# One forget gate, one conditioning step and one buffer: three re-orderings in a two-layer decoder trunk

## The chip, the cores and the metric

The kernel runs on one core of a Trainium2 chip. The metric is the device time of one execution in microseconds (us). The kernel before takes 3213.15 us, the median of three runs from 3211.61 to 3214.26. Engines are named as the profile names them: PE is TensorE (PEld its weight loads), DVE is VectorE, ACT is ScalarE, POOL is GpSimd, SP is SyncE, which issues most transfers ("SPq" is its queue).

## The reference

Two residual layers over a sequence of 512 tokens of width 1024, conditioned on a vector c. All data are fp32.

```
for layer in range(2):
    mod = silu(c) @ ada_w[layer] + ada_b[layer]        # 1024 x 6144
    sh1, sc1, g1, sh2, sc2, g2 = split(mod, 6)
    h = rmsnorm(x, norm_mix[layer]) * (1 + sc1) + sh1
    y = even_mixer(h) if layer == 0 else odd_mixer(h)
    x = x + g1 * y
    h = rmsnorm(x, norm_ffn[layer]) * (1 + sc2) + sh2
    x = x + g2 * peer_ffn(h)                           # 8 heads, 128 x 128 experts, top 16
out = rmsnorm(x, norm_final)

def odd_mixer(h):                                      # forgetting attention, 16 heads of 64
    q, k, v, f = split_cols(h @ w_in, (1024, 1024, 1024, 16))
    F = cumsum(log_sigmoid(f + b_forget))              # along the tokens
    s[t, u] = q[t] . k[u] / 8 + F[t] - F[u]            # causal
    return softmax(s) @ v @ w_out
```

The even mixer (sparse attention beside differential attention) and the expert stage are computed as well; of the expert stage only the first step, the normed and modulated input h, is touched by the change.

## The kernel before, in words

The 512 tokens are four blocks of 128 (NTB). A matmul of fp32 data is made as three products of fp32r pieces: `mm3` (L147 to L149) multiplies hi by hi, lo by hi and hi by lo. A tile is split into its pieces by `split_to`: ACT writes hi (L161, L164 with a scale) and DVE writes lo (L162, L165). In the profile wh and wl are the pieces of a weight chunk, kh, kl, qh, ql those of keys and queries, pth and ptl those of the transposed softmax.

**The ring.** The pool "stream" has three slots of 128x1024 under one tag, raw. Weight chunks (512 KB, L169, named raw), the slices of ada_w (256 KB, L237, named araw), the transposed forget logits fT, the triangle tri and a few others all take the next slot of this ring, so a load on SP's queue waits until an earlier user has let a slot go.

**The order of the work.** The program is written as generators. A list scheduler then sets the order on each engine, by its own estimates of when an instruction can start; the order in the code is where it starts from, not what it ends with.

**The odd mixer** (function `odd`) does this, in turn: the first half of v (1600 to 1644 us of the span); the forget logits (`proj_s` with chunk W[24], to 1650 us); the forget gate's chain: fT out of PSUM (L1002), four transposes (L1005), z = f + b (L1009), u = |z| (L1012), Exp (L1013), Ln (L1014), z again (L1015), the cumulative sum as four matmuls with a triangle of -1 (L1020), its split cum (L1022, L1023); then the second half of v with the chunks W[20] to W[23] (`proj_m`, 96 matmuls of 128x512, to 1682 us); then the attention, 1682 to 1898 us; then `mixer_out`, the output projection and the first steps of the expert stage.

**The attention** has 64 units, one for each of 16 heads and 4 token blocks, written out in four steps (`head_unit`): the scores (names sc), the causal mask (L1056, on DVE), the maximum mx (L474, DVE) and the exponential e (L477, ACT); the division (rc on DVE at L482, e at L808 on ACT); the transposes (tr, L495, PE) with pth (L497, ACT) and ptl (L500, DVE); and after the fourth block the product with v (pp) and oT (L818, ACT). Between the units `run_units` draws steps of two fillers: the projection of the q and k of the next pairs of heads, two 512 KB chunks for each group of eight units, and the list `bg`, from which it draws OB steps for each unit. In the odd mixer bg holds 64 steps of `ada` (L223 to L247): four of the six 1024-wide parts of mod, each as two halves of eight slices of ada_w. A step loads a slice (L237) and adds it, weighted, to adacc on DVE (L239 for a first slice, L241 for the others); after eight steps four matmuls (L245) sum adacc over the partitions and DVE writes mod (L247). With OB = 2 the steps are drawn in the first 32 of the 64 units.

**The expert stage's input.** For each token block `norm_block` writes xn (L299, with rstd from L288 to L290), and `h_steps` (L322) makes the modulated input: per half of the width four PE transposes (L330) of xn into PSUM, four scalings into hfull (L335 on ACT for b = 0 and 2, L337 on DVE for b = 1 and 3), and the split of hfull into h2h and h2l. hfull has one buffer, so a block waits for the split of the one before it. This happens at the end of mixer_out in both layers, ahead of the expert stage's first matmuls (named ups).

Of the kernel before, what the change touches and what calls it, by code (L numbers as in the profile page):

```python
# [7 lines left out]
F32 = mybir.dt.float32  # L8
# [9 lines left out]
P = 128  # L18
D = 1024
T = 512  # L20
# [41 lines left out]
OP = 1.8  # L62
OB = 2
OPP = 3
# [45 lines left out]
class Trunk:  # L110
    def __init__(self, tc, ctx, I, out):
        self.tc, self.nc, self.ctx, self.I, self.out = tc, tc.nc, ctx, I, out
        self.n = 0
        self.done = set()
        self.bg = []
        self.uw = []
        self.pin = False
        self.own = {}
        self.pending = {}
        self.banks = {"pp": 4, "sc": 2, "tr": 2, "s": 2, "u": 2, "g": 2, "q": 2, "ada": 1}  # L120
# [200 lines left out]
    def h_steps(self, tb, xn, cols, hT, pool, psum, tag):  # L321

        nc = self.nc
        a, sh = cols
        full = pool.tile([P, KT, P], F32, tag="hfull", name=self.nm("hfull"), bufs=1)
        for half in range(2):
            ps = self.bank(psum, tag)
            for b in range(4):
                kt = half * 4 + b
                nc.tensor.transpose(ps[:, b * P:(b + 1) * P], xn[:, kt * P:(kt + 1) * P], self.ident)  # L330
            for b in range(4):
                kt = half * 4 + b
                s = slice(b * P, (b + 1) * P)
                if b % 2 == 0:
                    nc.scalar.activation(full[:, kt], ps[:, s], AF.Identity, bias=sh[:, kt:kt + 1], scale=a[:, kt:kt + 1])  # L335
                else:
                    nc.vector.tensor_scalar(full[:, kt], ps[:, s], a[:, kt:kt + 1], sh[:, kt:kt + 1],  # L337
                                            op0=ALU.mult, op1=ALU.add)
            yield
            k = slice(half * 4, half * 4 + 4)  # L340
            t = slice(tb * P, (tb + 1) * P)
            self.split_to(hT[0][:, k, t], hT[1][:, k, t], full[:, k])
            yield
        return full
# [616 lines left out]
    def odd(self, layer):  # L961
        nc, I = self.nc, self.I
        W = I["odd_w"]
        with ExitStack() as s2:
# [28 lines left out]
            ep = s2.enter_context(self.pool("ep"))  # L993
            self.e_bufs = OEB
            with self.pool("fp") as fp:
                ps = self.bank(psum, "pp")
# [7 lines left out]
                for tb in range(NTB):  # L1004
                    nc.tensor.transpose(pf[:, tb * 16:(tb + 1) * 16], fT[:, tb * P:(tb + 1) * P], self.ident[:16, :16])  # L1005
                bf = fp.tile([P, 16], F32, name="bf")
                nc.scalar.dma_start(bf, I["odd_b_forget"].to_broadcast([P, 16]))
# [7 lines left out]
                nc.vector.scalar_tensor_tensor(z, z, 0.0, u, op0=ALU.min, op1=ALU.subtract)  # L1015
                tri = self.stream.tile([P, D], F32, tag="raw", name=self.nm("tri"))
                nc.sync.dma_start(tri[:, :T], I["ntri"])
                ps = self.bank(psum, "tr")
# [7 lines left out]
            def proj_qk(i):  # L1026
# [9 lines left out]
                for j in range(2):  # L1036
# [3 lines left out]

            self.proj_m([W[20 + c] for c in range(4)], hT, psum,
                        lambda tb, ps: self.split_to(vs[1][0][:, tb], vs[1][1][:, tb], ps))
            sq.close()
# [173 lines left out]
    def peer_enter(self, layer):  # L1217
# [9 lines left out]
        self.cols = self.mod_cols(layer, 1, self.hp)  # L1227
        self.xn = {}
        self.ssx = self.hp.tile([P, NTB, 2], F32, name=self.nm("ssx"))
        self.pad(self.hp, 96)  # L1230
# [15 lines left out]
    def peer(self, layer, last):  # L1246
# [7 lines left out]
        with ExitStack() as s1:  # L1254
            psum = s1.enter_context(self.pool("rps", bufs=2, space=PSUM))
            gls[0] = self.u_block(layer, 0)
            w = self.load_split(I["peer_wq"][layer, 0])
            self.peer_h(NDT, psum, "g")
            self.sn.close()
            for n in range(1, FIRST):  # L1260
# [315 lines left out]
```

## Time and profile before

| what | value |
|---|---|
| median of three runs | 3213.15 us (3211.61 to 3214.26) |
| profiled execution | 3209.09 us, its span 3206.9 us |
| mean granted TensorE clock | 0.988 |
| busy share of the span | PE 97%, DVE 80%, ACT 43%, POOL 22% |
| forget gate's chain | 1650 to 1660 us |
| attention of the odd mixer | 1682.3 to 1898.2 us |
| even mixer_out, end with h | to 375 us |
| odd mixer_out, end with h | to 1949 us |

The times of the trace are counted from the first instruction. A busy share is that of instructions in work on an engine. The granted clock is 1.00 at 2.4 GHz and 0.50 at 1.2 GHz, and a stretch between these values holds both. A row with "[idle before <-X]" names what the engine waited for.

### The profile page before, as it was taken

Reading aid. Unit: us, or ns where it says so; the run is one execution under the profiler, and the core shown is the slowest. Engines: PE = TensorE matmul, PEld = TensorE weight load, DVE = VectorE, ACT = ScalarE, POOL = GpSimd, SP = SyncE. Lnnn points to the kernel's source line nnn. Section 1 sums busy time; section 2 is a strip of 40 time slices with the busy share of each in tenths; the row PEclk is TensorE's granted clock in tenths of the full one; section 3 lists DMA queues with packets and bytes.
Section 4 is the critical chain, followed back from the end, with each engine's and each line's share of the span. In section 5 each row is a group of like instructions: output and inputs, shape, how many; then the busy total and the mean of one; then the engine's idle time right before and its main releaser. Section 6 shows DMA issues by size and latency. Waiting matters only on the chain.

```text
span 3206.9 us, 45322 instructions
## 1 busy us (share of the span) xinstructions
PE 3106.1 (97%) x16416; PEld 2689.4 (84%) x16416; DVE 2576.4 (80%) x5096; ACT 1367.1 (43%) x2276; POOL 705.8 (22%) x564
## 2 busy tenths in 40 slices
PE   8999899999999999999989999999999999999998
PEld 4766788998899999987867778899989999899877
DVE  6987799997687778788758767999867877778787
ACT  5567423553333333333445663255533333333333
POOL 0000000002344444434210000000024444444331
PEclk9999999999999999999999999999999999999999
DMA  7415523658799999999724422255688999999895
GB/s 242 132 60 178 173 86 107 228 224 289 269 334 322 319 336 333 317 329 320 238 101 159 138 86 79 92 178 224 214 289 296 332 327 324 322 320 319 311 324 196
DMA packets 304193, 758.92 MB, mean 237 GB/s; under 512 B 24456, under 2 KB 125376, under 8 KB 297824
## 3 DMA queue, kind: packets, MB, share of 16 engines
q1 hardware_dynamic: 225248, 480.04, 43.5%
q0 software_dynamic: 74240, 268.54, 23.2%
q10 hardware_dynamic: 4480, 7.44, 0.7%
q8 instruction: 129, 2.11, 0.3%
q14 instruction: 96, 0.79, 0.1%
HBM read 698.96 MB, written 56.64 MB: 236 GB/s over the span
## 4 chain that ended last, share of the span: by engine, by line
PE 67%; DVE 14%; DMA 13%; issue 3%; ACT 2%; POOL 0%; SPq 0%; DVEq 0%; ACTq 0%; POOLq 0%
PE ups L149 9%; PE ups L147 9%; PE ups L148 9%; PE y L148 8%; PE y L149 8%; PE y L147 8%; DMA gv<-in_peer_v_dram,eidx 5%; PE pp L147 3%; PE pp L149 3%; PE pp L148 3%; DMA araw<-in_ada_w_dram 2%; DVE wl L162 2%; DMA raw<-in_peer_v_dram 2%; PE gps L1210 1%; DMA gu<-in_peer_u_dram,eidx 1%
## 5 line engine op out<-in xcount | busy, mean ns | idle before, releaser
L161 ACT ACTIVATE wh<-raw 128x1024 fp32r<-128x1024 f32 x598 | 631.7, 1056 | 1007.8 <-PE ups L148 449.0
L162 DVE TENSOR_TENSOR wl<-raw,wh 128x1024 fp32r<-128x1024 f32 x598 | 729.5, 1220 | 140.0 <-ACT wh L161 139.0
L149 PE MATMUL ups<-h2h,wl 128*128 128x384 f32 x2048 | 693.7, 339 | 4.3 <-DVE wl L162 4.3
L147 PE MATMUL ups<-h2h,wh 128*128 128x384 f32 x2048 | 694.5, 339 | 3.1 <-ACT gl L1087 2.4
L148 PE MATMUL ups<-h2l,wh 128*128 128x384 f32 x2048 | 690.8, 337 | 0.0
L1447 POOL DMA_INDIRECT gu<-in_peer_u_dram,eidx x256 | 288.5, 1127 | 1637.6 <-DVE eidx L1306 1181.0
L147 PE MATMUL y<-wh,weh 128*128 128x512 f32 x1536 | 601.0, 391 | 11.3 <-ACT weh L161 9.4
L148 PE MATMUL y<-wl,weh 128*128 128x512 f32 x1536 | 603.7, 393 | 5.8 <-DVE wl L162 5.7
L149 PE MATMUL y<-wh,wel 128*128 128x512 f32 x1536 | 602.4, 392 | 0.0
L1447 POOL DMA_INDIRECT gv<-in_peer_v_dram,eidx x256 | 392.3, 1532 | 533.5 <-DVE gu L1454 333.5
L1462 DVE SCALAR_TENSOR_TENSOR acc<-gv,act,acc 128x1024 f32<-128x1024 f32 x256 | 328.2, 1282 | 165.7 <-DMA gv<-in_peer_v_dram,eidx 165.2
L147 PEld LDWEIGHTS ups<-h2h,wh 128*128 128x128 f32 x2048 | 386.6, 189 | 11.0 <-ACT gl L1087 3.0
L149 PEld LDWEIGHTS ups<-h2h,wl 128*128 128x128 f32 x2048 | 386.1, 189 | 7.5 <-DVE wl L162 7.5
L148 PEld LDWEIGHTS ups<-h2l,wh 128*128 128x128 f32 x2048 | 386.8, 189 | 6.5
L147 PEld LDWEIGHTS y<-wh,weh 128*128 128x128 f32 x1536 | 289.4, 188 | 71.1 <-ACT weh L161 10.7
L1454 DVE SCALAR_TENSOR_TENSOR gu<-gu,htm 128x1024 f32<-128x1024 f32 x256 | 312.1, 1220 | 45.2 <-DMA gu<-in_peer_u_dram,eidx 44.6
L148 PEld LDWEIGHTS y<-wl,weh 128*128 128x128 f32 x1536 | 289.2, 188 | 69.0 <-DVE wl L162 11.3
L161 ACT ACTIVATE weh<-wf 128x384 fp32r<-128x384 f32 x256 | 133.7, 524 | 497.9 <-PE y L148 356.9
L149 PEld LDWEIGHTS y<-wh,wel 128*128 128x128 f32 x1536 | 289.2, 188 | 61.2 <-DVE wel L162 1.3
L162 DVE TENSOR_TENSOR wel<-wf,weh 128x384 fp32r<-128x384 f32 x256 | 141.5, 553 | 82.0 <-ACT weh L161 81.7
L1341 DVE TENSOR_TENSOR wf<-gl,gt 128x384 f32<-128x384 f32 x256 | 140.2, 552 | 10.2 <-DMA gt<-gates 9.6
L1213 ACT ACTIVATE gst<-gps 128x512 f32<-128x512 f32 x192 | 104.1, 596 | 40.2 <-PE gps L1211 31.2
(411 smaller groups left out, 4272.0 us busy)
## 6 DMA issues: line engine op xcount, KB each, us to landing
raw<-in_peer_uT_dram SPq DMA_DIRECT2D x256, 512.0 KB
raw<-in_peer_v_dram SPq DMA_DIRECT2D x256, 512.0 KB
araw<-in_ada_w_dram SPq DMA_DIRECT2D x192, 256.0 KB
gates<-gst SPq DMA_DIRECT2D x48, 1024.0 KB
gt<-gates SPq DMA_DIRECT2D x32, 1536.0 KB
raw<-in_peer_wq_dram SPq DMA_DIRECT2D x32, 512.0 KB
raw<-in_odd_w_dram SPq DMA_DIRECT2D x25, 512.0 KB
raw<-in_even_w_dram SPq DMA_DIRECT2D x23, 512.0 KB
```

The source lines that it names most:

```text
L147: mm(out, a[0], b[0], start=start, stop=False)
L148: mm(out, a[0], b[1], start=False, stop=False)
L149: mm(out, a[1], b[0], start=False, stop=stop)
L161: self.lact = nc.scalar.activation(hi, src, AF.Copy)
L162: self.last = nc.vector.tensor_tensor(lo, src, hi.bitcast(F32), op=ALU.subtract)
L1210: nc.tensor.matmul(ps[:, z], oh[:, t, 1], og[:, t, 0], start=True, stop=False)
L1213: nc.scalar.activation(st[:, :, lt:lt + 4], ps.rearrange("p t i -> p i t"), AF.Copy, scale=1.0 / GSC)
L1341: nc.vector.tensor_tensor(wf.rearrange("p (c t) -> p c t", t=CT), gls[i].rearrange("p (c t) -> p c t", t=CT), self.gt[:, :, i % IG], op=AL ...
L1447: nc.gpsimd.indirect_dma_start(out=r, out_offset=None, in_=table, in_offset=bass.IndirectOffsetOnAxis(ap=eidx[:, k:k + 1], axis=0))
L1454: nc.vector.scalar_tensor_tensor(r, r, 1.0, htm, op0=ALU.mult, op1=ALU.mult, accum_out=act[:, k:k + 1])
L1462: nc.vector.scalar_tensor_tensor(acc, r, act[:, j:j + 1], acc, op0=ALU.mult, op1=ALU.add)
```

## The change

First, `proj_m` of the second half of v becomes a generator, `more`; the code draws VFILL = 14 of its steps between the gate's last z and the triangle matmuls, and the rest behind them. The load of the triangle is issued ahead of the gate's chain. A step of this generator holds three matmuls, one mm3. Second, OB is 1, so the 64 conditioning steps are drawn one a unit in all 64 units of the odd attention. Third, hfull has two buffers while the expert stage's input is made, in both layers, and under the same condition the scaling with b = 1 goes to ACT as well: three of four on ACT, one on DVE.

```diff
-OB = 2
+OB = 1
+VFILL = 14
...
+        self.hf_bufs = 1
...
-        full = pool.tile([P, KT, P], F32, tag="hfull", name=self.nm("hfull"), bufs=1)
+        full = pool.tile([P, KT, P], F32, tag="hfull", name=self.nm("hfull"), bufs=self.hf_bufs)
...
-                if b % 2 == 0:
+                if b % 2 == 0 or b < self.hf_bufs:
                     nc.scalar.activation(full[:, kt], ps[:, s], AF.Identity, bias=sh[:, kt:kt + 1], scale=a[:, kt:kt + 1])
                 else:
                     nc.vector.tensor_scalar(full[:, kt], ps[:, s], a[:, kt:kt + 1], sh[:, kt:kt + 1],
...
+            more = self.proj_m_steps([W[20 + c] for c in range(4)], hT, psum,
+                                     lambda tb, ps: self.split_to(vs[1][0][:, tb], vs[1][1][:, tb], ps))
             with self.pool("fp") as fp:
...
+                tri = self.stream.tile([P, D], F32, tag="raw", name=self.nm("tri"))
+                nc.sync.dma_start(tri[:, :T], I["ntri"])
                 bf = fp.tile([P, 16], F32, name="bf")
...
                 nc.vector.scalar_tensor_tensor(z, z, 0.0, u, op0=ALU.min, op1=ALU.subtract)
-                tri = self.stream.tile([P, D], F32, tag="raw", name=self.nm("tri"))
-                nc.sync.dma_start(tri[:, :T], I["ntri"])
+                for _ in range(VFILL):
+                    next(more)
                 ps = self.bank(psum, "tr")
...
-            self.proj_m([W[20 + c] for c in range(4)], hT, psum,
-                        lambda tb, ps: self.split_to(vs[1][0][:, tb], vs[1][1][:, tb], ps))
+            for _ in more:
+                pass
...
         self.xn = {}
+        self.hf_bufs = 2
...
             self.peer_h(NDT, psum, "g")
+            self.hf_bufs = 1
             self.sn.close()
```

Two lines more in the helpers and up to seven in `odd` shift the line numbers: L149 of before is L151, L161 is L163, L241 is L243, L1020 is L1027 and L1056 is L1063 in the changed kernel.

On PE, at the forget gate, before: the transposes of the logits, the four triangle matmuls (16x512 to 16x128), and then the first of the second half of v (wh_15673 is the piece of W[20]).

```order
L1005 MATMUL tr_15642<-ident,fT_15640 128x16 x4
L1020 MATMUL tr_15658<-tri_15656,z 16x512
L1020 MATMUL tr_15658<-tri_15656,z 16x384
L1020 MATMUL tr_15658<-tri_15656,z 16x256
L1020 MATMUL tr_15658<-tri_15656,z 16x128
L147 MATMUL pp_15667<-wh_15673,hTh_15199 128x512
```

The same place in the changed kernel.

```order
L1010 MATMUL tr_15642<-ident,fT_15640 128x16 x4
L1027 MATMUL tr_15716<-tri_15647,z 16x512
L1027 MATMUL tr_15716<-tri_15647,z 16x384
L1027 MATMUL tr_15716<-tri_15647,z 16x256
L149 MATMUL pp_15658<-wh_15664,hTh_15199 128x512
```

The fourth triangle matmul stands 42 matmuls later, among those of W[21] (wh_15694).

```order
L150 MATMUL pp_15659<-wl_15695,hTh_15199 128x512
L151 MATMUL pp_15659<-wh_15694,hTl_15200 128x512
L1027 MATMUL tr_15716<-tri_15647,z 16x128
L149 MATMUL pp_15660<-wh_15694,hTh_15199 128x512
L150 MATMUL pp_15660<-wl_15695,hTh_15199 128x512
```

Of the four only this last one has moved. On ACT, at the same place, in the changed kernel (u is the gate's chain; wh_15664, wh_15694, wh_15733 and wh_15763 are the pieces of W[20] to W[23]):

```order
L1007 ACTIVATE fT_15640<-pp_15609 16x512
L1019 ACTIVATE u<-z 128x64
L1020 ACT_TABLE_LOAD
L1020 ACTIVATE u<-u 128x64
L1021 ACT_TABLE_LOAD
L1021 ACTIVATE u<-u,ones 128x64
L163 ACTIVATE wh_15664<-raw_15662 128x1024
L163 ACTIVATE wh_15694<-raw_15692 128x1024
L163 ACTIVATE wh_15733<-raw_15731 128x1024
L163 ACTIVATE wh_15763<-raw_15761 128x1024
L1029 ACTIVATE cum<-tr_15716 16x512
```

Before, cum stands behind the second of these four splits; the first of them stands behind Ln in both kernels. On DVE, among the last of the 64 attention units, before:

```order
L1056 TENSOR_TENSOR sc_17897<-sc_17897,cmask 128x128
L482 RECIPROCAL rc_17887<-sums_17866 128x1
L500 TENSOR_TENSOR ptl_17726<-tr_17890,pth_17725 128x4x128
L474 TENSOR_REDUCE mx_17902<-sc_17897 128x1
L482 RECIPROCAL rc_17907<-sums_17885 128x1
L1056 TENSOR_TENSOR sc_17928<-sc_17928,cmask 128x128
L500 TENSOR_TENSOR ptl_17848<-tr_17910,pth_17847 128x128
L474 TENSOR_REDUCE mx_17933<-sc_17928 128x1
```

The corresponding stretch in the changed kernel:

```order
L1063 TENSOR_TENSOR sc_17907<-sc_17907,cmask 128x128
L484 RECIPROCAL rc_17917<-sums_17881 128x1
L502 TENSOR_TENSOR ptl_17811<-tr_17886,pth_17810 128x128
L476 TENSOR_REDUCE mx_17912<-sc_17907 128x1
L243 SCALAR_TENSOR_TENSOR adacc_17846<-araw_17925,cact,adacc_17846 128x512
L1063 TENSOR_TENSOR sc_17930<-sc_17930,cmask 128x128
L243 SCALAR_TENSOR_TENSOR adacc_17846<-araw_17949,cact,adacc_17846 128x512
L476 TENSOR_REDUCE mx_17935<-sc_17930 128x1
L484 RECIPROCAL rc_17940<-sums_17915 128x1
L502 TENSOR_TENSOR ptl_17811<-tr_17920,pth_17810 128x2x128
```

About one adacc stands between two masks where there was none, and in the first half of the units one where there were two. On DVE, at the end of the odd mixer_out, around xn of the third token block (xn_18452; hfull_18418 and h2l are of the second block, yt and x_3093 of the fourth), before:

```order
L337 TENSOR_SCALAR hfull_18418<-tr_18430,a_col_18090,mod 128x128
L288 TENSOR_SCALAR rstd_18453<-ssx_18092 128x1
L162 TENSOR_TENSOR h2l_18079<-hfull_18418,h2h_18078 128x4x128 x2
L544 TENSOR_TENSOR yt_18506<-pp_18458,row_18119 128x512
L545 TENSOR_TENSOR x_3093_15191<-x_3093_15191,yt_18506 128x512
L290 RECIPROCAL rstd_18453<-rstd_18453 128x1
L299 TENSOR_SCALAR xn_18452<-x_3092_15190,rstd_18453 128x1024
```

The same in the changed kernel.

```order
L339 TENSOR_SCALAR hfull_18418<-tr_18419,a_col_18090,mod 128x128
L164 TENSOR_TENSOR h2l_18079<-hfull_18418,h2h_18078 128x4x128
L339 TENSOR_SCALAR hfull_18418<-tr_18430,a_col_18090,mod 128x128
L292 RECIPROCAL rstd_18453<-rstd_18453 128x1
L546 TENSOR_TENSOR yt_18506<-pp_18458,row_18119 128x512
L164 TENSOR_TENSOR h2l_18079<-hfull_18418,h2h_18078 128x4x128
L301 TENSOR_SCALAR xn_18452<-x_3092_15190,rstd_18453 128x1024
```

The second half of the second block's h2l now stands between yt and xn, and x of the fourth block behind xn.

## Rows read from the trace of the kernel before

**Rows 1.** The whole span by engine: busy us, share, instructions.

```profile
PE 3106.1 (97%) x16416; PEld 2689.4 (84%) x16416; DVE 2576.4 (80%) x5096; ACT 1367.1 (43%) x2276; POOL 705.8 (22%) x564
```

**Rows 2.** Busy time by stretch, eight attention units each: stretch, length, engines, granted clock, DMA share.

```profile
1682.30:1718.30 36.00, 33.06 (x171) 27.31 (x172) 28.12 (x60) 19.25 (x44) 1.08 (x2) 1.00 0.43 140
1718.30:1747.60 29.30, 26.89 (x126) 21.53 (x125) 24.59 (x56) 17.54 (x41) 1.07 (x2) 0.88 0.56 173
1747.60:1774.10 26.50, 24.53 (x135) 19.56 (x134) 23.69 (x55) 16.63 (x40) 1.07 (x2) 1.00 0.54 176
1774.10:1805.70 31.60, 27.59 (x134) 22.26 (x132) 25.86 (x61) 17.54 (x42) 1.08 (x2) 0.89 0.59 183
1805.70:1832.40 26.70, 26.26 (x137) 21.64 (x136) 19.42 (x46) 19.98 (x44) 1.07 (x2) 0.94 0.30 99
1832.40:1855.40 23.00, 22.71 (x121) 18.52 (x120) 16.01 (x39) 17.48 (x42) 1.07 (x2) 1.00 0.18 57
1855.40:1876.60 21.20, 19.99 (x109) 16.15 (x108) 14.07 (x37) 16.39 (x40) 0.00 (x0) 1.00 0.11 39
1876.60:1898.20 21.60, 16.38 (x83) 12.08 (x84) 14.28 (x40) 17.22 (x45) 0.00 (x0) 1.00 0.10 35
```

**Rows 3.** Chain of waits by line, first 32 units, then the last 32.

```profile
by line: DMA araw<-in_ada_w_dram 16.8%; DMA raw<-in_odd_w_dram 13.8%; DVE adacc L241 9.8%; PE pp L147 6.0%; PE pp L149 5.6%; PE pp L148 5.4%; DVE wl L162 4.6%; DVE mx L474 4.1%; issue 4.0%; ACT wh L161 3.5%; PE tr L245 3.4%; PE tr L495 2.6%
...
by line: PE pp L148 15.3%; PE pp L147 14.3%; PE pp L149 14.3%; PE tr L495 6.3%; ACT e L808 5.3%; DVE mx L474 4.8%; ACT e L477 4.6%; DMA raw<-in_odd_w_dram 4.6%; ACT pth L497 4.2%; PE sc L147 3.2%; ACT wh L161 3.2%; PE sc L148 3.1%; PE sc L1
```

**Rows 4.** Waits in the first 32 units, then the last 32: total us, times, longest.

```profile
ACT e L477 <- DVE mx L474: 17.5, 17, 3.5
DVE adacc L241 <- DMA araw<-in_ada_w_dram: 6.8, 13, 1.8
...
ACT e L477 <- DVE mx L474: 4.9, 10, 1.0
```

**Rows 5.** Groups of instructions by line and shape, first 32 units.

```profile
L241 DVE SCALAR_TENSOR_TENSOR adacc<-araw,cact,adacc 128x512 f32<-128x512 f32 x56 | 41.8, 747 | 7.4 <-DMA araw<-in_ada_w_dram 6.8
L245 PE MATMUL tr<-ones,adacc 128*128 128x1 f32 x56 | 8.5, 272 | 0.1
```

**Rows 6.** PE in order of time around 1777 us: start, us, instruction.

```profile
1776.82 0.77 PE L147 MATMUL sc<-kh,qh 128*128 128x512 f32 x1 [2.22 <-ACT e L477]
```

**Rows 7.** The attention's three stretches at half clock, columns as in rows 2.

```profile
1732.50:1739.30 6.80, 6.80 (x23) 5.73 (x24) 6.52 (x16) 5.02 (x13) 0.54 (x1) 0.50 0.42 130
1776.90:1783.70 6.80, 6.80 (x23) 5.91 (x24) 5.12 (x12) 3.97 (x9) 0.54 (x1) 0.50 0.50 157
1807.60:1811.00 3.40, 3.21 (x10) 2.62 (x11) 2.53 (x7) 2.75 (x8) 0.00 (x0) 0.50 0.72 229
```

**Rows 8.** The forget gate in order of time.

```profile
1651.55 0.26 ACT L1012 ACTIVATE u<-z 128x64 f32<-128x64 f32 x1 [0.77 <-DVE z L1009]
1654.94 1.99 ACT L161 ACTIVATE wh<-raw 128x1024 fp32r<-128x1024 f32 x2
1655.35 4.45 PE L1020 MATMUL tr<-tri,z 128*16 128x512 f32 x8 [4.09 <-DVE z L1015]
```

**Rows 9.** PE at the end of both mixer_out, even then odd.

```profile
370.83 1.97 PE L330 MATMUL tr<-ident,xn 128*128 128x128 f32 x8 [3.93 <-DVE hfull L337]
374.75 0.90 PE L330 MATMUL g<-ident,xn 128*128 128x128 f32 x3 [1.96 <-DVE hfull L337]
...
1944.49 1.94 PE L330 MATMUL tr<-ident,xn 128*128 128x128 f32 x8 [2.47 <-DVE rstd L288]
1948.60 0.90 PE L330 MATMUL g<-ident,xn 128*128 128x128 f32 x3 [2.17 <-DVE hfull L337]
```

**Rows 10.** DVE at the end of the odd mixer_out, in order of time.

```profile
1942.06 0.69 DVE L544 TENSOR_TENSOR yt<-pp,row 128x512 f32<-128x512 f32 x1 [0.44 <-PE pp L149]
1943.59 0.75 DVE L299 TENSOR_SCALAR xn<-x,rstd 128x1024 f32<-128x1024 f32 x1
1946.16 0.41 DVE L337 TENSOR_SCALAR hfull<-tr,a_col,mod 128x128 f32<-128x128 f32 x1 [1.68 <-ACT hfull L335]
```

## Prediction

> **What bounds the kernel now.** I read the page's busy shares first: PE works 97% of the span [rows 1], so the change can only win where PE stands still or is slowed, and that is in a few stretches. I then cut the odd mixer's attention by stretches of eight units, between the starts of every eighth causal mask [rows 2]. The reader is to see two halves. The first four stretches take 123.4 us, the last four 92.5 us, for the same number of units. In the first half PE is idle 36.00 - 33.06 = 2.94, 2.41, 1.97 and 4.01 us, together 11.3 us, and the granted clock falls below 1.00 in two stretches; in the second half it is idle 0.44, 0.29, 1.21 and 5.22 us. DVE works 78 to 89% of the time in the first half and 66 to 73% in the second. Third, the chain of waits in each half [rows 3]: in the first the loads and additions of the conditioning sums (araw, raw, adacc) hold 40% of it, in the second no such line leads and PE's own products do. The waits by engine say the same [rows 4]: ACT's exponential waited 17.5 us for DVE's maximum in the first half, 4.9 us in the second. So the first half goes at the pace of the ring and of DVE, and the second nearly at that of PE.
>
> The other two places are the forget gate, where PE stands 4.09 us [rows 8], and the ends of both mixer_out, where it stands 3.93 and 1.96 us, then 2.47 and 2.17 us [rows 9].
>
> **OB = 1.** Nothing is added or taken away: 64 slices are loaded and added, one instead of two to a unit. What moves is about half of them, from the first four stretches into the last four. For DVE a slice costs 0.747 us [rows 5], and seven of them with 0.747 us are 5.2 us a stretch (the eighth, which opens a sum, is shorter). For PE half of the 8.5 us of the sums' matmuls [rows 5], 4.2 us, moves.
>
> The first four stretches then lose three things. The 4.2 us of PE. The half clock: two stretches of 6.80 us in which PE is busy 6.80 us at half clock [rows 7], of which half, 6.8 us together, is what the clock costs. Ahead of one of them PE waited 2.22 us for the exponential [rows 6], which waits for the maximum, which stands behind adacc on DVE. And idle time: DVE falls from 28.1, 24.6, 23.7 and 25.9 us to 22.9, 19.4, 18.5 and 20.7 us [rows 2], and the ring has 10 loads for eight units instead of 18, so a slice is no longer waited for (6.8 us of DVE waits now [rows 4]). PE's idle time there should come near the 0.65 us a stretch of the fifth to seventh (mean of 0.44, 0.29 and 1.21). I take twice that, 1.25 us, since DVE stays somewhat fuller: 11.3 - 5.0 = 6.3 us. Together -4.2 - 6.8 - 6.3 = -17.3 us.
>
> The last four pay. PE gets 4.2 us. The one short fall of the clock there (3.21 us busy at half clock [rows 7]) gives back 1.6 us. DVE goes from 19.4, 16.0 and 14.1 us to 24.6, 21.2 and 19.3 us in stretches five to seven, about as full as the second to fourth are now, with 2.8 us of PE idle each (2.41, 1.97, 4.01). Their idle time then lies between 0.65 us (nothing lost) and 2.8 us; the middle, 1.7 us, is +3.2 us for three. In the eighth stretch no projection is left to cover a wait and PE is idle 5.2 us already; 5.2 us of additions between masks, maxima and divisions cost between 0 and 5.2 us, and I take 3.5 us, nearer to the upper end because DVE works in order and every unit passes through it three times or more. Together 4.2 - 1.6 + 3.2 + 3.5 = +9.3 us. OB is worth -17.3 + 9.3 = -8.0 us, with -19.7 + 2.6 = -17 us at one end (idle 0.65 us everywhere, nothing paid at the tail) and, at the other, the rivals below.
>
> Where I put the clock back to 1.00, there is a rule against it. The row shows a wait of 2.22 us right before the clock fell at 1776.9 us [rows 6, 7], and the eighth stretch, idle for a quarter of its time at clock 1.00 [rows 2]. The Trainium skill, TensorE: Matmul & The Clock Gate, section "HAM oscillation — how this bites in real kernels", says that bursts of matmuls parted by waits send the clock back to half again and again. By that rule the waits that OB moves into the second half would take the falls along with them, and the sum would lack the 6.8 us; by the eighth stretch's row it keeps them. The trace agrees with the rule at 1777 us and not in the eighth stretch.
>
> **The forget gate.** The code draws 14 steps of v ahead of the triangle, but the order on PE shows three of the four triangle matmuls still ahead of v, waiting for z, and on ACT the split of W[20] still behind Ln. In the trace that split starts 1654.94 us, as Ln ends, and the triangle 1655.35 us [rows 8]. PE has nothing to do between the transposes and z in either order, so the 4.09 us stay. The fourth triangle matmul, 128 of 1280 columns, moves behind v's products: of the 4.45 us that is a tenth, 0.45 us, at half clock, and half that at full clock; v fills its place at half clock. That is -0.2 us. The triangle's load goes ahead of the gate on SP's queue, and the loads of W[22] and W[23] wait for other slots of the ring. What is late next is cum, queued on ACT behind two more splits, some 10 us later, and POOL's copies of it into the keys behind that; their users are the first scores, which come after all of v, and v hides them. If that cover were gone it would cost up to 10 us; I give it 0. Bounds -4.1 (the stall goes after all) and +1.
>
> **hfull.** Four scalings for half a block are 0.41 us each on DVE [rows 10], and by the row they hand over to ACT and back, so moving one in four to ACT shortens nothing by itself. The second buffer frees a block from the split of the one before, 1.29 us in two pieces at most, which is the gain's bound: -1.3 us a layer. On the other side, in the odd layer xn of the third block now stands behind a piece of h2l. DVE now goes from yt at 1942.06 us to xn at 1943.59 us [rows 10], and PE's transposes wait for it until 1944.49 us [rows 9]; later scalings on ACT and 0.65 us of h2l between could put it up to 1.3 us later, at half clock. In the even layer the fourth block's transposes leave the place ahead of the first expert matmuls, a little gain. I take -0.2 us there and +0.7 us here, +0.5 us, with -3 and +3 as ends.
>
> **Sum.** -8.0 - 0.2 + 0.5 = -7.7 us. The profiled execution took 3209.09 us, 4.06 us less than the median; 3201.4 us there is 3205.4 us against the median of 3213.15.
>
> **Rivals.**
>
> (A) The attention packs to PE's pace: -17 us, 3196 us. For it: PE's work in the eight stretches is 197.4 us, less 8.4 us of half clock, so 189 us against 215.9 us. Against it: no stretch with DVE over 80% has PE idle under 1.9 us.
>
> (B) It is given back: stretches five to seven take the 2.8 us idle of the second to fourth (+6.4 us), the eighth the full 5.2 us, the clock falls once more for 6.8 us (+3.4 us); 4.2 - 1.6 + 6.4 + 5.2 + 3.4 = +17.6 us against -17.3 us: 3213 us, no change. For it: DVE at 87% in these stretches. Against it: the ring, which held the first half's chain, is no longer short.
>
> (C) Slower: DVE's additions stand in the way of every unit, and each stretch of the second half grows by the whole 5.2 us, +20.9 us, while the first half gains only the 4.2 us of matmuls, one of the two clock falls and half the idle time, -4.2 - 3.4 - 3.1 = -10.7 us. Sum +10.2 us, 3223 us. It decides once the last four stretches take over 110 us together. For it: DVE's idle time in the second half, 7 us a stretch, is made of waits in its own queue, which additions don't fill if they are late. Against it: they have ten loads' time to be early.
>
> (D) The gate's stall of 4.09 us goes as the code says, so -12 us in all, 3201 us. Against it: the order on PE and ACT.
>
> **How the numbers follow.** I give the forecast (-3 to -12 us; by itself 3201 to 3210 us) 0.43, (A) 0.20, (B) 0.22, (C) 0.10, (D) 0.05. A measurement of this kernel tells about 0.2% from no change, 6.4 us: below 3206.7 us is faster, above 3219.6 us slower. Of the forecast 0.27 lies on the faster side; with (A) and (D) that is 0.52. The rest of it, 0.16, with 0.20 of (B) is 0.36 for the same. (C) with what is left of (B) is 0.12. The range from 3196 to 3215 us leaves out (C) and the far side of (A).
>
> **What would show it.** In the profile after: the first four stretches at 104 to 110 us and the last four at 98 to 106 us; the clock at 1.00 in the first half; araw's share of the chain there under half of 16.8%; ACT's wait for the maximum balanced over both halves; PE still idle about 4 us ahead of the triangle; the first expert matmuls within 1 us of 375.4 and 1949.3 us, counted from the end of each mixer's projection. I am wrong if the second half takes more than 110 us, if the clock falls there as often as it did in the first, or if the gain lies at the gate or at hfull.

## The result, and the profile after

The changed kernel takes 3195.65 us, the median of five runs (3191.37 to 3199.46); before, measured beside it, takes 3211.61 us (3207.43 to 3214.26). The ratio is 0.995, with a 95% interval from 0.9935 to 0.9964: 16 us faster, between 12 and 21. A second chip gave 3193.24 against 3208.18 us, a ratio of 0.9953 (0.9936 to 0.9971). The direction was forecast, but only half of the size: 7.7 us were forecast, to 3205.4 us, and the measured time lies just below the range that ends at 3196 us.

The profiled execution took 3195.65 us, its span is 3193.9 us. I cut its attention as in [rows 2], at the start of every eighth mask (the last stretch here ends with the first matmul of the output projection; in before that is at 1895.97 us, so 19.4 us after its last mark at 1876.6). Columns as in [rows 2]: busy time of PE, PEld, DVE, ACT and POOL, then the granted clock, the DMA share and GB/s.

```profile
1682.60:1719.90 37.30, 33.87 (x165) 26.91 (x164) 25.65 (x54) 21.03 (x46) 1.07 (x2) 1.00 0.28 92
1719.90:1744.40 24.50, 22.68 (x127) 19.08 (x127) 19.57 (x48) 17.56 (x40) 1.08 (x2) 1.00 0.43 130
1744.40:1766.90 22.50, 22.17 (x127) 19.04 (x126) 19.47 (x48) 17.40 (x40) 1.07 (x2) 1.00 0.44 141
1766.90:1789.80 22.90, 22.19 (x125) 18.70 (x124) 19.60 (x48) 17.31 (x40) 1.08 (x2) 1.00 0.42 138
1789.80:1813.20 23.40, 22.65 (x130) 19.28 (x130) 19.31 (x48) 17.19 (x40) 1.07 (x2) 1.00 0.43 136
1813.20:1836.00 22.80, 22.30 (x123) 18.63 (x122) 19.34 (x47) 17.23 (x40) 1.08 (x2) 1.00 0.42 139
1836.00:1859.80 23.80, 22.28 (x130) 18.90 (x129) 18.51 (x46) 16.66 (x39) 0.00 (x0) 1.00 0.34 111
1859.80:1884.30 24.50, 18.30 (x84) 13.63 (x83) 19.18 (x50) 16.91 (x41) 0.00 (x0) 0.86 0.40 128
```

From the second on the stretches are now alike, 22.5 to 24.5 us; the first also holds the start. The two falls of the clock in the first half are gone. In stretches five to seven DVE went from 66 to 73% up to 78 to 85% of the time, and PE is idle there only 0.75, 0.50 and 1.52 us. The last stretch is the one that pays: its clock is 0.86. The first four take 107.2 us, as the prediction's signs had it (104 to 110); the last four take 94.5 us, less than the 98 to 106 us that it named.

The chain of waits, by line, in the first 32 units of the changed kernel, against the first line of [rows 3], and the two waits of [rows 4] in the same stretch:

```profile
by line: DMA raw<-in_odd_w_dram 19.0%; PE pp L151 9.7%; PE pp L150 8.9%; PE pp L149 8.5%; DMA araw<-in_ada_w_dram 6.1%; ACT wh L163 5.9%; DVE adacc L243 5.3%; PE tr L497 4.6%; ACT e L479 4.0%; DVE wl L164 3.4%; DVE mx L476 2.6%; PE tr L247 
```

```profile
ACT e L479 <- DVE mx L476: 12.1, 17, 1.8
DVE adacc L243 <- DMA araw<-in_ada_w_dram: 2.8, 3, 2.1
```

araw fell from 16.8 to 6.1% of the chain, and PE's products now lead with the loads of the projections' weights (raw). ACT's wait for the maximum is balanced, 12.1 us in the first half and 10.5 us in the second.

At the forget gate the wait has not changed, as the order on PE and ACT let expect. PE in time, against [rows 8], and below it, with the columns of [rows 2], the stretch at half clock there:

```profile
1651.66 0.42 PE L1010 MATMUL tr<-ident,fT 16*128 16x16 f32 x4 [0.68 <-ACT fT L1007]
1656.17 4.00 PE L1027 MATMUL tr<-tri,z 128*16 128x512 f32 x6 [4.09 <-DVE z L1022]
```

```profile
1653.20:1660.00 6.80, 3.83 (x6) 0.73 (x6) 2.59 (x3) 4.51 (x6) 0.00 (x0) 0.50 0.30 107
```

The wait is 4.09 us in both kernels. At the ends of both mixer_out, against [rows 9]:

```profile
365.61 0.66 PE L332 MATMUL tr<-ident,xn 128*128 128x128 f32 x4 [1.91 <-DVE hfull L339]
369.23 1.94 PE L332 MATMUL tr<-ident,xn 128*128 128x128 f32 x8 [2.96 <-DVE rstd L290]
372.77 1.01 PE L149 MATMUL ups<-h2h,wh 128*128 128x384 f32 x2 [1.60 <-ACT h2h L163]
...
1933.38 1.94 PE L332 MATMUL tr<-ident,xn 128*128 128x128 f32 x8 [2.92 <-DVE xn L301]
1936.93 1.01 PE L149 MATMUL ups<-h2h,wh 128*128 128x384 f32 x2 [1.61 <-ACT h2h L163]
```

The waits of 3.93, 1.96 and 2.17 us are now 2.96, 1.60 and 1.61 us; the odd layer's for xn grew from 2.47 to 2.92 us, as the prediction had it, but the next one shrank more.

**A table by stage.** Whole times scatter by 10 us and more: the two stretches from the first expert matmul of a layer, to the gate's transposes and to the end, whose loops the change doesn't touch, took 2533.0 us together in the profile of before, 2535.8 and 2542.5 us in two of the changed kernel and 2524.8 us in that of OB = 1 alone. The stages between repeat better: in the kernels whose attention is as before, the first 32 units took 104.3 to 106.6 us, the next 24 70.9 to 73.0 us, the stage ahead of them 47.8 to 49.3 us, and the others agree within 0.1 us, but for the odd layer's last (6.0 to 6.5 us with the same edits). Most of what follows is read from these. Each length is a difference of two starts or ends on PE or DVE in one profiled execution:

| stage, us | before | changed | changed, again | OB alone | gate alone | hfull alone |
|---|---|---|---|---|---|---|
| even layer, last product of mixer_out to first expert matmul | 11.44 | 9.60 | 9.60 | 11.44 | 11.45 | 9.60 |
| logits' transposes to first mask | 48.75 | 46.61 | 46.42 | 46.20 | 48.62 | 47.81 |
| 1st to 33rd mask | 106.08 | 91.51 | 91.06 | 92.31 | 104.34 | 105.74 |
| 33rd to 57th mask | 70.94 | 70.07 | 69.16 | 69.47 | 71.23 | 71.00 |
| 57th mask to output projection | 19.37 | 24.48 | 24.20 | 24.49 | 19.37 | 19.37 |
| output projection | 46.05 | 46.14 | 46.16 | 46.10 | 46.05 | 46.12 |
| odd layer, last product to first expert matmul | 7.24 | 6.46 | 6.02 | 7.17 | 7.24 | 6.47 |
| sum | 309.87 | 294.87 | 292.62 | 297.18 | 308.30 | 306.11 |

By the stages this pair of executions gained 15.0 us, the second profile 17.3 us; the medians say 16. The 2.1 us ahead of the first mask are no gain by themselves: 55 instead of 64 products of the projections (pp<-hTh,wh and its like, 0.23 us apiece) stand there, and the others behind that mask.

### The profile page after: what moved, and what is told of

It is laid out like the page before. It is cut to its first block, busy times and chain, and to the rows that moved or that the text cites. A ratio compares the mean times of both kernels' runs of the same rounds, so it can differ in the third digit from the quotient of the medians.

```text
span 3193.9 us, 45290 instructions
## 1 busy us (share of the span) xinstructions
PE 3093.7 (97%) x16416; PEld 2681.5 (84%) x16416; DVE 2569.9 (80%) x5080; ACT 1372.6 (43%) x2292; POOL 706.7 (22%) x564
## 4 chain that ended last, share of the span: by engine, by line
PE 62%; DMA 16%; DVE 14%; issue 3%; ACT 3%; POOL 0%; SPq 0%; DVEq 0%; ACTq 0%; POOLq 0%
PE ups L151 8%; PE ups L149 8%; PE ups L150 8%; PE y L150 7%; PE y L151 7%; PE y L149 7%; DMA gv<-in_peer_v_dram,eidx 7%; DVE wl L164 3%; PE pp L151 3%; PE pp L149 3%; PE pp L150 3%; DMA raw<-in_peer_v_dram 2%; DMA araw<-in_ada_w_dram 2%; DMA gu<-in_peer_u_dram,eidx 2%; PE gps L1217 1%
## 5 line engine op out<-in xcount | busy, mean ns | idle before, releaser
L163 ACT ACTIVATE wh<-raw 128x1024 fp32r<-128x1024 f32 x598 | 631.4, 1056 | 1008.1 <-PE ups L150 474.2
L151 PE MATMUL ups<-h2h,wl 128*128 128x384 f32 x2048 | 693.8, 339 | 7.1 <-DVE wl L164 6.8
L149 PE MATMUL ups<-h2h,wh 128*128 128x384 f32 x2048 | 693.6, 339 | 5.6 <-ACT h2h L163 3.2
L149 PE MATMUL y<-wh,weh 128*128 128x512 f32 x1536 | 601.4, 392 | 9.6 <-ACT weh L163 8.6
L151 PE MATMUL y<-wh,wel 128*128 128x512 f32 x1536 | 602.9, 393 | 0.0
L149 PEld LDWEIGHTS ups<-h2h,wh 128*128 128x128 f32 x2048 | 386.1, 189 | 13.8 <-ACT h2h L163 4.0
L151 PEld LDWEIGHTS ups<-h2h,wl 128*128 128x128 f32 x2048 | 385.6, 188 | 11.3 <-DVE wl L164 11.1
L163 ACT ACTIVATE weh<-wf 128x384 fp32r<-128x384 f32 x256 | 133.6, 524 | 504.5 <-PE y L150 370.2
L149 PEld LDWEIGHTS y<-wh,weh 128*128 128x128 f32 x1536 | 289.8, 189 | 69.3 <-ACT weh L163 9.9
L151 PEld LDWEIGHTS y<-wh,wel 128*128 128x128 f32 x1536 | 289.3, 188 | 60.6 <-DVE wel L164 0.7
L1094 ACT ACTIVATE gl<-ups 128x384 f32<-128x384 f32 x256 | 121.3, 474 | 0.1
```

What stands on the lines that cost most here:

```text
L149: mm(out, a[0], b[0], start=start, stop=False)
L151: mm(out, a[1], b[0], start=False, stop=stop)
L163: self.lact = nc.scalar.activation(hi, src, AF.Copy)
L1094: nc.scalar.activation(gl, ps[:, :ND], AF.Gelu_apprx_tanh)
```

## The experiments

**One part alone, three kernels.** OB first.

```diff
-OB = 2
+OB = 1
```

> The kernel before with OB = 1 and nothing else. Theory: the gain of the whole change, 16 us by the medians, is OB's, and my price for the second half of the attention (+9.3 us) was too high by about 5 us. Then this kernel is 11 to 14 us faster than before (3198 to 3201 us where before is 3212). By the prediction's own sum it would be 8 us. Rival: the other two parts carry a third of the gain or more; then OB alone gives under 9 us.

Ratio 0.9967 (0.995 to 0.9985), which is 5 to 16 us; the medians are 3196.06 us against 3210.32 us on that chip. By the table it is 12.7 us, of which 2.5 come ahead of the first mask, 13.8 in the first 32 units and 1.5 in the next 24, and 5.1 are paid in the last eight. So OB carries most of the gain, and the price of the second half was too high.

The second is the part of hfull: `self.hf_bufs = 2` with the third scaling on ACT.

> The kernel before with the two buffers of hfull and the third scaling on ACT, nothing else. Theory: the even layer's first expert matmuls come 2 to 3 us earlier (372.8 instead of 375.4 us) and the odd layer's 0 to 1 us, so 2 to 4 us faster. The prediction's sum said 0.5 us slower. Rival: the early start is given back in the expert stage, since in the changed kernel the odd gate came 0.8 us later than before although the expert stage began 2.65 us earlier; then within 1 us of before.

Ratio 1.0001 (0.9986 to 1.0016): the whole time can't tell. The stages can: -1.84 us in the even layer, the same in every kernel with this part, and -0.77 in the odd (-0.8 to -1.2 in the others). So by the stages not slower by 0.5 us, but 2.6 us faster, of which the odd layer's part is the less certain: a kernel below without this part took 6.88 us there. Whether the expert stage gives it back is not shown. The 2.65 us by which the expert stage began earlier in the changed kernel was a coincidence, though: two kernels without this part began it at 372.9 and 373.0 us, and this one at 373.7 us.

The third is the gate's part, with OB = 2 and one buffer.

> The kernel before with the forget gate's part of the change (OB = 2, one buffer for hfull). Theory: PE stands about 4.1 us ahead of the triangle as before, since three of four triangle matmuls still stand ahead of v and the split of W[20] behind Ln, and the time is within 1 us of before. Rival: the slots of the ring and the later cum speed up or slow down the first attention units, 2 us or more either way.

Ratio 1.001 (0.9994 to 1.0026). From the transposes to the first mask -0.13 us, far inside the scatter of that stage, and PE's wait ahead of the triangle is there as before: the part does nothing that can be seen.

**Ring or DVE?** Two kernels with OB = 2 take one load each from the first half. The first leaves DVE the additions of 64 of 512 columns.

```diff
-  nc.vector.scalar_tensor_tensor(acc, raw, self.cact[:, kt:kt + 1], acc, ...)
+  nc.vector.scalar_tensor_tensor(acc[:, :64], raw[:, :64], self.cact[:, kt:kt + 1], acc[:, :64], ...)
```

> The kernel before (OB = 2), but in the odd attention the additions of the slices on DVE take 64 of 512 columns, so the conditioning of the second layer is wrong; every slice is still loaded through the ring. Two theories of why the first 32 attention units are slow. The ring: each slice needs one of three slots and takes its turn; then the first 32 units stay within 4 us of their 106 us (from the first mask to the 33rd) and the time within 4 us of before. DVE: the additions stand ahead of masks, maxima and lo pieces; then taking away some 33 us of DVE work brings the 32 units to under 96 us, and the time falls by 10 us or more.

From the first to the 33rd mask 102.25 us, 3.8 less than in the profile of before and 2.1 less than the shortest with its attention; ratio 0.9985 (0.9969 to 1.0002). That is within the ring's 4 us and far from DVE's 96 us. Its stretches two to four:

```profile
1719.20:1745.10 25.90, 23.33 (x125) 19.69 (x125) 17.15 (x55) 16.36 (x40) 1.29 (x2) 0.93 0.62 195
1745.10:1773.70 28.60, 24.27 (x136) 19.74 (x135) 19.36 (x57) 17.15 (x41) 1.08 (x2) 1.00 0.58 184
1773.70:1801.00 27.30, 25.37 (x133) 20.48 (x132) 18.32 (x56) 17.00 (x40) 1.07 (x2) 0.94 0.61 194
```

DVE is down to two thirds of the time, as in the second half of before, and yet PE is idle 2.57, 4.33 and 1.93 us, as much as in [rows 2]. The chain of its first 32 units says why:

```profile
by line: DMA araw<-in_ada_w_dram 40.5%; DMA raw<-in_odd_w_dram 10.7%; issue 7.1%; DVE adacc L241 4.8%; ACT wh L161 4.4%; PE tr L245 4.2%; DVE wl L162 4.1%; DVE kl L162 2.3%; DVE mx L474 2.3%; DVE sc L1056 2.0%; PE sc L147 1.8%; DVE ql L165 
```

With DVE light, the slices' loads alone hold 40% of the chain. What was gained is mostly clock: 6.8 us at half instead of 13.7 us are worth 3.4 of the 3.8 us. The second kernel leaves DVE all its additions and halves the loads: each slice is added twice.

```diff
-  else:
+  elif kt % share == 0:                  # share = 2
       raw = self.stream.tile([P, D], F32, tag="raw", name=self.nm("araw"))[:, :T]
-  nc.sync.dma_start(raw, self.I["ada_w"][layer, m, kt, :, s])
+  if kt % share == 0:
+      nc.sync.dma_start(raw, self.I["ada_w"][layer, m, kt, :, s])
```

> The kernel before (OB = 2), but in the odd attention every slice of ada_w that is loaded is added twice and the next is not loaded, so the conditioning of the second layer is wrong; DVE does as many full additions as before, the ring carries 32 slices instead of 64. Theory (the ring): the first 32 units, from the first mask to the 33rd, fall from 106 us to the changed kernel's 92 us or near it (91 to 97 us), and PE's idle time in stretches two to four from 8.4 us to under 4 us, with DVE as full as before. Rival (DVE): they stay over 102 us.

98.61 us, 7.5 less than before; the expected band ended at 97, so the ring is not all of it. Ratio 0.9967 (0.9953 to 0.998). Its stretches two to four:

```profile
1722.90:1747.60 24.70, 23.17 (x128) 19.02 (x128) 23.07 (x53) 16.21 (x39) 1.08 (x2) 1.00 0.36 119
1747.60:1774.00 26.40, 24.45 (x133) 19.29 (x132) 24.06 (x56) 16.77 (x40) 1.08 (x2) 1.00 0.36 120
1774.00:1800.50 26.50, 24.64 (x133) 19.31 (x133) 23.98 (x56) 17.09 (x41) 1.08 (x2) 1.00 0.39 131
```

DVE is busy 90 to 93% of the time, more than before, and PE is idle 1.53, 1.95 and 1.86 us, 5.3 us together instead of 8.4 (under 4 were expected), with the clock at 1.00 throughout. The ring was the larger part, DVE the smaller: of the 5.5 us by which PE's idle time fell in the changed kernel, half the loads alone give 3.1, and all of the clock in this one execution. Whether the three slots or the rate at which slices land make the ring short is not separated: no run has a fourth slot.

**What do DVE's additions cost once the ring is free?** The changed kernel, with every slice added twice on DVE, in one execution.

```diff
+  for _ in range(2):
       nc.vector.scalar_tensor_tensor(acc, raw, self.cact[:, kt:kt + 1], acc, ...)
```

> The changed kernel with every slice after the first of a sum added twice on DVE, so the conditioning of the second layer is wrong; loads, PE and ACT as in the changed kernel. DVE, 19 us of 23 in a stretch of eight units, gets 5.2 us more. Theory: DVE costs nothing until its own work fills the stretch, and is a plain bound from there: stretches of 25 to 26.5 us, so 100 to 106 us from the first mask to the 33rd (91.5 in the changed kernel) and 74 to 80 us for the next 24 units (70). Rival, the prediction's price (2.8 us of PE idle time at 82 to 89%, and more above): over 82 us for the 24 units.

95.39 us to the 33rd mask and 75.67 us for the next 24 units: 3.9 and 5.6 us more than in the changed kernel, for some 13 us more of DVE in each. The first figure is below the band, the second within. Stretches five and six:

```profile
1798.10:1823.60 25.50, 23.91 (x126) 18.75 (x125) 23.71 (x55) 16.76 (x40) 1.08 (x2) 1.00 0.39 125
1823.60:1849.00 25.40, 23.64 (x125) 18.53 (x124) 23.66 (x54) 16.76 (x40) 1.08 (x2) 1.00 0.38 126
```

DVE is 93% busy and PE idle 1.6 to 1.8 us. So fullness alone is cheap: one addition of every slice, which takes DVE to 78 to 85%, left stretches five to seven with 0.3 us more of PE's idle time each, and the second, to 93%, made each some 1.9 us longer. It is no plain bound either, since the price begins below a full stretch. The last eight units do pay: 29.47 us instead of 24.48, so 5.0 us for the second addition as 5.1 us for the first. The make-up differs: the first brought 1.0 us of PE's idle time and a fall of the clock, the second 3.6 us of idle time.

**Which part of hfull?** One execution each, the buffer alone and the third scaling on ACT alone; the edits are shown against the kernel with both.

```diff
-  if b % 2 == 0 or b < self.hf_bufs:     # buffer alone
+  if b % 2 == 0:
```

> The kernel before with the second buffer of hfull alone; two of four scalings stay on DVE. Theory: the buffer is what shortens the way from the last product of mixer_out to the first expert matmul (11.44 us before and 9.60 us with both edits in the even layer, 7.24 and 6.47 us in the odd), since a block's scalings no longer wait for the split of the block before; then about 9.6 and 6.5 us. Rival: it is the third scaling on ACT, or the order that the scheduler sets with it; then over 11 and 7 us.

9.93 and 6.59 us: the buffer gives 1.51 of the 1.84 us in the even layer and 0.65 in the odd.

```diff
-  bufs=self.hf_bufs                       # scaling alone
+  bufs=1
```

> The kernel before with the third scaling on ACT alone, hfull in one buffer. Theory (the buffer does it): 11.2 to 12 us and 7.2 to 8 us. Rival: about 9.6 and 6.5 us.

11.20 and 6.16 us. In the even layer the theory holds. In the odd layer it fails: the scaling alone gives 1.08 us, within the 0.8 to 1.2 us of both together, so there the gain does not hang on the buffer. What the scheduler's other order does there I have not taken apart.

**A gate that is filled, from the changed kernel.**

```diff
+  next(more)                                    # splits W[20]
+  with self.tc.issue_after(self.lact.ins):
       nc.scalar.activation(fT, ps[:16], AF.Copy)
   ...transposes of fT
+  for _ in range(7):
+      next(more)
+  lead = self.lmm.ins                           # the last matmul of the eighth step
   ...z, u, z
-  for _ in range(VFILL):
-      next(more)
+  with self.tc.issue_after(lead):
       nc.tensor.matmul(ps[:16, sb * P:], z[:, sb], tri[:, :T - sb * P], ...)
```

> The changed kernel with the gate filled in earnest: W[20] is split on ACT ahead of fT, eight steps of v (24 matmuls) stand on PE behind the transposes and the triangle is held behind them. Theory: PE's 4.1 us ahead of the triangle go, and with them the fall of the clock at 1653 us; from the logits' transposes to the first mask it takes 40 to 43 us instead of 46.6, so the kernel is 4 to 6 us faster than the changed one (3190 us where that is 3195.65). Rival: z comes later because fT, the table loads and z wait behind the split, or W[21] is late; then under 2 us.

39.56 us, 7.05 less than the changed kernel; 3187.07 us where that took 3193.24 us, ratio to before 0.9939 (0.9925 to 0.9953). PE at the triangle, and the same stretch with the columns of [rows 2]:

```profile
1655.58 0.42 PE L1012 MATMUL tr<-ident,fT 16*128 16x16 f32 x4
1655.93 0.50 PE L150 MATMUL pp<-wl,hTh 128*128 128x512 f32 x1
...
1660.71 2.33 PE L1031 MATMUL tr<-tri,z 128*16 128x512 f32 x8
```

```profile
1655.60:1663.00 7.40, 7.40 (x34) 4.70 (x33) 2.69 (x4) 5.32 (x7) 0.00 (x0) 1.00 0.23 71
```

No row here has a wait, and the four triangle matmuls take 2.33 us instead of 4.45, at clock 1.00. The stall was 4.1 us and the triangle's half clock 2.1 us. The other 0.9 us are no gain: four products of v stand ahead of the transposes here, outside the stage. That leaves 6.1 us, and the medians say 6.2, a little over the 4 to 6 us expected. With the last kernel below it is the fastest that was tried, by the medians faster than both the one before and the changed one.

**The tail.** The changed kernel with `OB = 1.25`:

> The changed kernel with OB = 1.25: the 64 steps fall into the first 52 units and leave the last 12 alone. Theory: the last stretch (from the 57th mask to the output projection's first matmul, 24.5 us) comes back to the 19.4 us of before, with no fall of the clock there, and the ring still has room (12 loads for eight units); 3 to 5 us faster than the changed kernel. Rival: 12 loads are already too many, the first half loses 3 us or more and the sum is nothing.

The last stretch did come back, to 19.39 us, but the stage ahead of the first mask took 48.72 us, the first 32 units 94.47 and the next 24 71.40 us: 234.0 us for the four, where the changed kernel took 232.7 and 230.8 us. Ratio 0.9972 (0.996 to 0.9983). The rival holds: the first half lost the 3 us. The other try keeps the filled gate and draws eight steps in the second half of v:

```diff
-  for _ in more:
-      pass
+  self.bg = [self.ada(layer, m, ah, psum, "tr", 0) for m in (2, 4, 3, 5)]
+  for i, _ in enumerate(more):
+      if i % 3 == 0 and i < 24:
+          self.step()
```

> The kernel with the gate filled in earnest, and eight of the 64 conditioning steps drawn in the second half of v, where DVE is busy under a third of the time, so that the attention has 56 steps for 64 units and its last eight none. Theory: the last stretch comes back from 23.4 to 19.4 us and v grows by less than 1 us: 3 to 4 us faster than 3187 us. Rival: the eight slices take the ring from W[21] to W[23] and from the first keys and queries; from the logits' transposes to the first mask it takes 43 us or more instead of 39.6, and nothing is won.

44.22 us ahead of the first mask, 4.7 more; 88.38 and 69.36 us for the units and 21.71 for the last eight. The four stages sum to 223.67 us with it and 223.69 without; 3186.84 us, ratio 0.9936 (0.9917 to 0.9954). The last stretch didn't come back to 19.4 us; what it and the first 32 units lost came back ahead of the first unit. The rival holds here too.

> The changed kernel once more, on the same chip as the two beside it, for comparison: 0.995 of before, with its stretches of eight units between 22.5 and 24.5 us but for the first.

That run is the column "changed, again" of the table: 0.9953 (0.9936 to 0.9971).

## Why the prediction was wrong

**The first four stretches: right.** Forecast -17.3 us, of matmuls, clock and idle time; measured, from the logits' transposes to the 33rd mask, -2.1 - 14.6 = -16.7 us, with nine products of the projections, 2.0 us, more than before in this part; without them -18.7 us. The clock stayed at 1.00 and PE's idle time in stretches two to four fell from 8.4 to 2.9 us.

**Stretches five to seven: the step that failed.** The prediction read from [rows 2] that DVE at 82 to 89% goes with 2 to 4 us of PE idle time a stretch, and let these stretches take the middle, 1.7 us each. With the sums' matmuls (three quarters of 4.2 us) and the clock's 1.6 us back, that was +4.8 us; measured were -0.9 us (-1.8 in the second profile). The idle time grew by 0.8 us, not by 3.2, so 2.4 of the 5.7 us of miss are this step. Another 2.0 us are those nine products: 135 instead of 144 stood in these stretches, the others ahead of the 33rd mask, which moves time and gains none. The rest lies in PE's other work, among it the sums' matmuls, which brought 2.5 us instead of 3.2. DVE, too, came out less full than the prediction had it, 57.2 us for the three stretches instead of 65.1: the additions brought 15.0 us, but three splits of weights and other work stood elsewhere.

The rows didn't carry the step: in stretches two to four a full DVE and a short ring stood together, and idle time was put down to the one that the busy column shows. The kernels part them. PE's mean idle time a stretch, over stretches two to four, with the ring short: 2.8 us with DVE at 85% (before) and 2.9 us at 67% (light). With the ring free: 1.8 us with DVE at 92% (half the loads), 1.5 us at 94% (every slice added twice) and 1.0 us at 84% (changed). The prediction had named the ring as the holder of the first half's chain [rows 3] (its 40% for the conditioning sums counts raw, the projections' weights, among them; without it they hold 26.6%), and then priced the second half as if DVE had held it. By the stages the whole forecast missed by 7.3 us: 4.3 us in the attention with the gate, most of it here, and 3.1 us at hfull, with 0.1 us the other way at the output projection.

**The last stretch: right in size, by luck.** +1.05 + 3.5 = +4.6 us forecast, +5.1 us measured. But the 3.5 us were to be waits, and PE's idle time grew only from 5.2 to 6.2 us: most of the rest is a new fall of the clock, from 1875.1 us. Ahead of it PE waited 1.86 us for a ptl that stands behind an addition on DVE and behind dg (1.22 us), which is made from the finished mod and stood in the fifth stretch before:

```profile
1874.92 1.77 PE L247 MATMUL tr<-ones,adacc 128*128 128x1 f32 x8 [1.86 <-DVE ptl L502]
```

```profile
1875.10:1881.80 6.70, 6.01 (x23) 4.98 (x23) 3.45 (x5) 2.69 (x4) 0.00 (x0) 0.50 0.25 77
```

6.01 us of work at half clock are 3.0 us of cost. The rule that the prediction weighed, from the Trainium skill, TensorE: Matmul & The Clock Gate, section "HAM oscillation — how this bites in real kernels", by which the falls go along with the waits, agrees with the trace here and at 1776.9 us [rows 6]. It does not cover all falls: right ahead of the one at 1732.5 us [rows 7] PE's longest wait was 0.81 us, and in the kernel with half the loads the last stretch, with the work that it had before, took 20.80 us instead of 19.37, of which 3.4 us at half clock, after a wait of 1.26 us that before had too. The falls of the first half didn't move into stretches five to seven, where PE's longest wait was 1.16 us; that the missing waits are the reason is not shown.

**The gate: right in the mechanism.** The order showed that the stall stays, and it stayed. The forecast of -0.2 us is too small to be tested: measured were -0.13 us in a stage that scatters by 1.5 us. What the prediction didn't say is what the stall is worth: 6 us, with its clock.

**hfull: the wrong sign.** Forecast +0.5 us, measured -2.6. The term was summed from the scalings' order and gave the buffer nothing but a bound of -1.3 us a layer. That bound was too low as well: the buffer alone gave 1.5 us in the even layer. The wait for it was in the trace. ACT in the even layer, before:

```profile
368.34 0.46 ACT L335 ACTIVATE hfull<-tr,mod,a_col 128x128 f32<-128x128 f32 x1 [1.06 <-DVE h2l L162]
```

ACT stood 1.06 us until the split of the block before had left hfull, at PE's longest wait [rows 9]. The prediction read PE's row, whose releaser is DVE's hfull, and didn't follow it one step further back. The later xn in the odd layer, for which it charged, did happen (2.92 instead of 2.47 us) and was outweighed.

**The rivals.** (A), 3196 us, comes nearest in time, but by luck and not by its mechanism: the tail pays 5.1 us, and 2.6 us are hfull's. (B) and (C) fell with stretches five to seven. (D) fell; the stall stays until W[20] is split ahead of fT.

## What to carry to other kernels

Where two shared things are short in the same stretch, the busy column shows the engine and not the buffer: before a move is priced by an engine's fullness, look for a stretch in which it is full and the other thing is not, or make one. A fill that is drawn at the right place in the code fills nothing if its own first operand (here the split of a weight on ACT) still stands behind the chain that it is to cover. And background work on a shared engine was cheapest where foreground work was plenty: here 5 us of additions in a stretch of eight units brought 0.3 us of idle time on PE in the middle of the attention, and cost 5 us in its last eight units, 3 of them by the clock.

## What was not expected of the hardware

DVE at 93% held PE up by under 2 us in 25, although every unit passes through it several times. The two expert stages together varied by 18 us between profiled executions in which their code was the same, several times the effect of two of the three parts. And a wait of 1.86 us ahead of a run of single-column matmuls came with a fall of the clock worth 3 us, while the last stretch of before, idle for a quarter of its time, kept 1.00, and the same stretch behind half the loads did not. What decides it no run here shows.
